# Latent attention on one Trainium2 core: softmax denominators as a product with ones, reciprocals out of PSUM, maxima turned by a product with the identity

## The chip, the cores and the metric

The kernel runs on one core of one Trainium2 chip. The core has a matrix engine (TensorE, PE in the profile; its weight loads are PEld), a vector engine (VectorE, DVE), an activation engine (ScalarE, ACT), a general engine (GpSimd, POOL) and a queue that issues DMAs (SyncE, SP). PE writes only to PSUM, which has eight banks of 512 fp32 columns on 128 partitions; in this kernel POOL works on SBUF, and DVE and ACT read PSUM.

The metric is the device time of one execution in microseconds, as the median of repeated runs. One execution is also profiled; a unit's timeline comes from it.

## The reference, cut to what matters

The model has two layers on 1024 latent and 256 context tokens of width 1024: windowed attention, then multi-head latent attention. The change touches the core of the second layer. It has 16 heads; the scores of a head are the sum of a 64-wide product and a 32-wide rotary product, over 1280 keys (256 context and 1024 latent):

```python
def attend(qn, qr, kn, kr, v):
    s = (jnp.einsum("bqhd,bkhd->bhqk", qn, kn)
         + jnp.einsum("bqhd,bkd->bhqk", qr, kr)).astype(F32) * scale
    p = jax.nn.softmax(s, axis=-1).astype(v.dtype)
    return jnp.einsum("bhqk,bkhd->bqhd", p, v)
...
yx = (ox * jax.nn.silu(gx)) @ w_out
```

The softmax needs each query's maximum before the exponentials and each query's sum after them. The result of a head is multiplied by a gate and goes into the output product.

## The kernel before, in words

**Units.** The second layer's attention runs as 32 units (`UnitB`), one for each head and half of the queries: pair of heads, head `e` in the pair, half, in the order `i = 4 * pair + 2 * e + half`. A unit has 512 queries.

**Steps of a unit.** `prep` loads the unit's queries from DRAM with eight DMAs. `top(b)`, b = 0 to 3, computes the scores of 128 queries against all keys with the queries on the partitions (line 1322 into `psm`, two PSUM banks, for the first 1024 keys; line 1330 into `rest`, columns 256 to 511 of banks 0 and 1, for the last 256 keys, in `top(1)` and `top(2)` only, for two blocks at once), and DVE takes negated maxima (lines 1324, 1331) into one column per block of the tile `mx`; `top(3)` joins the two kinds of maxima (line 1333). `shift` turns the four columns into rows by a PE transpose into `pm_bank` (bank 1, columns 0 to 127; line 1337), and DVE and ACT place them as extra rows of the query operand (lines 1338, 1343). `score(i)`, i = 0 to 4, computes the scores again with 256 keys on the partitions (line 1359, as two products side by side), so that the shifted scores land in one of two two-bank `slots`; `expo` takes the exponential on ACT (line 1365) into a ring of six tiles and POOL adds the tiles up into `acc`, a [128, 512] tile whose sum over partitions is the denominator (lines 1369, 1373). `PV` is the value product (line 1381), ten products of 512 columns whose stationary operand has 64 columns; they go in pairs into the lower and the upper half of the partitions of bank 0 (`pv_bank`). `fin` and `fin1` add the two halves (ACT line 1396, DVE line 1400) into the unit's part of `o`; for e = 1 `fin1` also issues the load of the gate.

**Denominators.** `fin2` turns `acc` by four PE transposes into a bank of a slot (line 1410), so that the queries lie on the partitions, and DVE sums along the free dimension (line 1411). For e = 1 DVE takes the reciprocals of both heads, [128, 8] (line 1414), and ACT spreads them to 64 columns (line 1419). One iteration later, `fin3` turns them back with four transposes (line 1425), DVE multiplies `o` of both heads (line 1426), POOL multiplies with the gate (line 1428), and a DMA stores the result to `og_d` (line 1429).

**Order of work.** PE, ACT and DVE run in the order in which the program is written (`manual_schedule`); each engine takes its instructions strictly in that order. POOL and the SP queue are ordered by the framework. The loop over `ui` staggers three units: in iteration `ui` the unit `u` is scored, its predecessor `pu` gets its value product and finish, and the next two units (`nu`, `nnu`) get their maxima. On PE an iteration is: `score(0)` around `nu.top(2)`, `score(1)`, `nu.top(3)`, in some iterations `make_K` (keys of the next pair, for `ui % 4` of 0 or 1), `pu.PV`, `nu.shift`, `ppu.fin3` (after odd `e`), `pu.fin2`, in iterations 8, 16 and 24 `make_V` (values of the next heads), `nnu.top(0)`, `score(2)`, `score(3)`, `nnu.top(1)`, `score(4)`. On DVE `fin1` stands behind the maximum of `nnu.top(0)` and ahead of that of `nnu.top(1)`; in iterations 8, 16 and 24 it stands ahead of `make_V`. The generators `wo_fill` and `out_fill` place pieces of the output weights' preparation and of the output product, which follows.

Of the kernel before, what the change touches and what calls it, by code (L numbers as in the profile page):

```python
# [14 lines left out]
AX = mybir.AxisListType  # L15
# [32 lines left out]
def shp(ap, *dims):  # L48
    n = 1
    for d in dims:  # L50
        n *= d
    ap = ap[:, 0:n]
    if len(dims) == 1:
        return ap
    names = "abcdefg"[: len(dims)]
    kw = {c: d for c, d in zip(names[1:], dims[1:])}
    return ap.rearrange("p (" + " ".join(names) + ") -> p " + " ".join(names), **kw)
# [3 lines left out]
def kernel(ctx: ExitStack, tc: tile.TileContext, t, out, dbg=None):  # L61
    nc = tc.nc
# [4 lines left out]
    PB = ppool.tile([128, 8, 512], F32, name="PB")  # L67
    R = cpool.tile([128, int(R_KB * KB)], F32R, name="arena_r")
    F = cpool.tile([128, F_KB * KB], F32, name="arena_f")
    ident = cpool.tile([128, 128], F32, name="ident")  # L70
# [21 lines left out]
    def f_at(kb, *dims):  # L92
        n = int(np.prod(dims))
        return shp(F[:, int(kb * KB) : int(kb * KB) + n], *dims)
# [177 lines left out]
    sm_ring8 = SmallRing(6, 8)  # L272
# [279 lines left out]
    rbr = Ring(F, [42, 47], 256)  # L552
# [26 lines left out]
    class UnitA:  # L579
# [96 lines left out]
        def fin2(self, fast=False):  # L676
            g, og = self.g, self.og
            o = self.o
            rt = shp(prt(), 4, 128)
            for j in range(2):  # L680
                nc.tensor.transpose(rt[:, j, :], self.rb[:, j * 128 : j * 128 + 128], ident)
            rs = shp(rtr.next(), 2, 128)
            nc.scalar.copy(rs, rt[:, 0:2, :])
            eng = nc.vector if fast else nc.gpsimd
            eng.tensor_mul(rs, rs, self.gt)
            eng.tensor_mul(o, o, rs)
            hi = og[:, 0, 2 * g : 2 * g + 2, :]
            eng.tensor_copy(hi, o)
            eng.tensor_sub(og[:, 1, 2 * g : 2 * g + 2, :], o, hi.bitcast(F32))  # L689
# [23 lines left out]
    units = [UnitA(ti, g) for ti in ORDER for g in range(4)]  # L713
# [46 lines left out]
    class RawRing:  # L760
        i = 5

        def next(self):
            self.i += 1
            return raw[:, self.i - 1, :]
# [104 lines left out]
    for c in range(2):  # L870
        ps = proj_t(1, 0, c)
# [14 lines left out]
    for bi in (8, 9):  # L886
        for c in range(2):
            ps = proj_t(bi, 0, c)
# [268 lines left out]
    for ti in range(NT):  # L1157
        n = ti + 3
# [50 lines left out]
    glr = Ring(R, [60, 62], 512)  # L1209
    warm = sm(1)  # L1210
    otr = Ring(F, [0, 4], 1024)
    rbr = Ring(F, [8, 9], 256)
    mxr = Ring(F, [44, 44.5], 128)
    psm = PB[:, 2:4, :]
    pm_bank = PB[:, 1, 0:128]
    slots = [PB[:, 4:6, :], PB[:, 6:8, :]]
    pv_bank = PB[:, 0, :]
    rest = PB[:, 0:2, 256:512]

    def slot():  # L1220
        slots.reverse()
        return slots[1]
# [67 lines left out]
    class UnitB:  # L1290
# [43 lines left out]

        def shift(self):
            pm, r2 = pm_bank, self.q[2]
            nc.tensor.transpose(pm[0:100], self.mx[:, 0:100], ident)
            nc.vector.tensor_mul(
                shp(r2[32:36], 4, 128),
                pm[32:36].unsqueeze(1).to_broadcast([4, 4, 128]),  # L1340
                ident[32:36, 32:36].unsqueeze(2).to_broadcast([4, 4, 128]),
            )
            nc.scalar.copy(r2[96:100], r2[32:36].bitcast(F32))
# [41 lines left out]
        def fin(self):  # L1385
            if self.e == 0 and self.half == 0:
                UnitB.o = shp(otr.next(), 2, 512)
                UnitB.dens = {}
            if self.e == 0:
                UnitB.dens[self.half] = shp(sm_ring8(), 2, 4)  # L1390
            self.den = UnitB.dens[self.half]
            self.o = UnitB.o[:, self.half, :]
            pv = self.pv
            a, b2 = (slice(0, 64), slice(64, 128)) if self.e == 0 else (slice(64, 128), slice(0, 64))
            self.a = a
            nc.scalar.copy(self.o[a], pv[b2])
# [7 lines left out]
                    out=self.gt.bitcast(F32), in_=g1_d[self.pair, :, self.half * 512 : self.half * 512 + 512]  # L1404
                )

        def fin2(self, pd):
            pd = shp(pd, 4, 128)
            for b in range(4):
                nc.tensor.transpose(pd[:, b, :], self.acc[:, b * 128 : b * 128 + 128], ident)  # L1410
            nc.vector.reduce_sum(self.den[:, self.e, :], pd, AX.X)
            if self.e == 0:
                return
            nc.vector.reciprocal(self.den, self.den)
            rec = self.den.rearrange("p e b -> p b e").unsqueeze(3)
            self.rbs = []
            for b in range(0, 4, 2):
                rb = shp(rbr.next(), 2, 2, 64)
                nc.scalar.copy(rb, rec[:, b : b + 2].to_broadcast([128, 2, 2, 64]))
                self.rbs.append(rb)  # L1420

        def fin3(self, rt):
            for b in range(4):
                rb = self.rbs[b // 2][:, b % 2].rearrange("p e d -> p (e d)")
                nc.tensor.transpose(rt[:, b * 128 : b * 128 + 128], rb, ident)
            nc.vector.tensor_mul(self.o, self.o, rt)
            eng = nc.vector if self.i == NU - 1 else nc.gpsimd
            eng.tensor_mul(self.o, self.o, self.gt.bitcast(F32))
            load(out=og_d[self.pair, :, self.half * 512 : self.half * 512 + 512], in_=self.o)
# [114 lines left out]
    units = [UnitB(i) for i in range(NU)]  # L1544
    vk = make_V(0, slots[0], slots[1])
    for m in mxr.bufs:
        nc.vector.memset(m, 0.0)
    for p in range(1, 3):
        g_tile(8, p)
    g_tile(9, 1)  # L1550
# [7 lines left out]
    with tc.manual_schedule(engines={E.PE, E.Activation, E.DVE}):  # L1558
        kr = make_kr()
        ones_kr()  # L1560
        next(kr)
        next(kr)
        g_tile(8, 3, 0, pv_bank)
        next(kr)
        g_tile(8, 3, 1)
        make_K(0, (0, 1), slot())
        g_tile(9, 3, 0, psm[:, 0])
        make_K(0, (2,), slot())
        g_tile(9, 3, 1)
        next(vk)  # L1570
        u0.top(0)
        next(vk)
        g_tile(8, 4, 0, slots[0][:, 0])
        u0.top(1)
        next(vk)
        u0.top(2)
        g_tile(8, 4, 1)
        units[2].prep()
        u0.top(3)
        g_tile(9, 4, 0, slots[0][:, 1])  # L1580
        u0.shift()
        u1.top(0)
        make_K(1, (0, 2), slots[1])
        u1.top(1)
        g_tile(9, 4, 1)
        nc.scalar.activation(warm, const[:, 1:2], AF.Exp)
        u1.top(2)
        for ui, u in enumerate(units):
            pu, ppu = [units[ui - n] if ui >= n else None for n in (1, 2)]
            nu, nnu = [units[ui + n] if ui + n < NU else None for n in (1, 2)]  # L1590
            if nnu and ui:
                nnu.prep()
            if ui == 0:
                u.score(0)
                nu.top(3)
                u.score(1)
                nu.shift()
                nnu.top(0)
                u.score(2)
                u.score(3)  # L1600
                nnu.top(1)
                u.score(4)
                continue
            u.score(0, 0, 2)
            if nu:
                nu.top(2)
            u.score(0, 2, 5)
            u.score(1, hold=True)
            if nu:
                nu.top(3)  # L1610
            x = slot()
            if ui % 4 == 0 and u.pair < 7:
                make_K(u.pair + 1, (0, 2), x)
            if ui % 4 == 1 and u.pair < 7:
                make_K(u.pair + 1, (1,), x)
            if ui == NU - 2:
                next(out_fill)
            pu.PV()
            u.expo(1)
            if ui % 4 > 1 and ui < 23 or ui > 25:  # L1620
                next(wo_fill)
            if ui == NU - 1:
                next(out_fill)
            pu.fin()
            if nu:
                nu.shift()
            if ppu and ppu.e == 1:
                ppu.fin3(x[:, 0])
            pu.fin2(x[:, 1])
            if ui % 8 == 0:  # L1630
                pu.fin1()
                for _ in make_V(u.pair // 2, x):
                    pass
            if nnu:
                nnu.top(0)
            if ui % 8:
                pu.fin1()
            u.score(2)
            u.score(3)
            if nnu:  # L1640
                nnu.top(1)
            u.score(4)
        u, pu = units[-1], units[-2]
        pu.fin3(slot()[:, 0])
        next(out_fill)
        next(out_fill)
        u.PV()
        u.fin()
        u.fin1()
        next(out_fill)  # L1650
        next(out_fill)
        u.fin2(slot()[:, 0])
        next(out_fill)
        next(out_fill)
        u.fin3(slot()[:, 0])
    for _ in out_fill:
        pass

# [73 lines left out]
```

## Time and profile before

| | |
|---|---|
| median of 3 runs | 1577.26 us (1575.3 to 1577.57) |
| the profiled execution's own time | 1574.73 us |
| its span | 1573.0 us |
| granted TensorE clock, mean | 0.995 |
| PE busy | 1538.7 us, 98% |
| DVE busy | 993.5 us, 63% |
| ACT busy | 772.8 us, 49% |
| POOL busy | 753.8 us, 48% |

A line of a group in the profile names the source line, the engine, the operation, the tiles written and read, shapes and count; then the busy time, the mean duration of one in ns, and the idle time of the engine just ahead of it with what ended it. `PB` is PSUM, `arena_f`, `arena_r` and `arena_k` are SBUF. A timeline line has the start in us, the length in us, engine, line and operation; neighbouring equal instructions are merged (x4), and idle time ahead stands in brackets. Many lines share line 128 to 130, the helper for products split into three.

### The profile page before, as it was taken

What the parts mean: (1) busy time and instruction counts of PE and PEld (TensorE: products, weight loads), DVE (VectorE), ACT (ScalarE), POOL (GpSimd) and SP (SyncE); (2) the same over time, 40 slices, a digit from 0 to 9 for tenths busy, and PEclk for the clock granted to TensorE, in tenths of its full rate; (3) what the DMA queues carried; (4) which work ended last, traced back from release to release, by engine and by line L of the source; (5) the groups of instructions that cost most, each with busy time, mean ns of one, the idle gap of its engine ahead of it and who ended that gap; (6) DMA issues with size and microseconds to landing.
All of it is one profiled execution on the core that took longest, in us unless ns stands there. A gap on an engine that the chain in (4) does not pass through costs nothing.

```text
span 1573.0 us, 26868 instructions
## 1 busy us (share of the span) xinstructions
PE 1538.7 (98%) x9846; PEld 1228.6 (78%) x9846; DVE 993.5 (63%) x1757; ACT 772.8 (49%) x1492; POOL 753.8 (48%) x810
## 2 busy tenths in 40 slices
PE   7999999999999999998999999999999999999998
PEld 4988888887878888888998899666766766766687
DVE  3878996657777777768425203666567566567354
ACT  4432322267777777767313323455555555555322
POOL 1151211136564444544105140588688688689410
PEclk9999999999999999999999999999999999999999
DMA  8357774653343222345105753313233233244251
GB/s 316 114 159 219 199 207 137 200 164 99 99 146 100 85 89 85 95 132 182 48 1 156 262 151 98 91 45 98 61 98 101 71 91 88 61 138 113 69 168 68
DMA packets 148277, 192.83 MB, mean 123 GB/s; under 512 B 13985, under 2 KB 86177, under 8 KB 148145
## 3 DMA queue, kind: packets, MB, share of 16 engines
q1 hardware_dynamic: 146672, 188.94, 40.2%
q10 hardware_dynamic: 1472, 2.16, 0.5%
q8 instruction: 78, 1.28, 0.3%
q14 instruction: 55, 0.44, 0.1%
HBM read 144.90 MB, written 46.15 MB: 121 GB/s over the span
## 4 chain that ended last, share of the span: by engine, by line
PE 81%; DVE 8%; issue 3%; DMA 3%; ACT 2%; POOL 2%; SPq 0%; DVEq 0%; POOLq 0%; ACTq 0%
PE PB L128 12%; PE PB L129 12%; PE PB L130 12%; PE PB L1359 12%; PE PB L1381 9%; PE PB L621 5%; PE PB L662 5%; PE PB L1322 4%; PE PB L652 4%; DVE arena_f L193 2%; DVE arena_f L519 1%; DMA arena_f<-a_w_in 1%; PE PB L1330 1%; PE PB L1410 1%; ACT arena_r L123 1%
## 5 line engine op out<-in xcount | busy, mean ns | idle before, releaser
L128 PE MATMUL PB<-arena_r 128*128 128x512 f32 (+3 forms) x1216 | 410.8, 339 | 5.5 <-ACT arena_r L423 2.4
L129 PE MATMUL PB<-arena_r 128*128 128x512 f32 (+3 forms) x1184 | 395.2, 334 | 1.8 <-POOL arena_r L689 0.8
L130 PE MATMUL PB<-arena_r 128*128 128x256 f32 (+3 forms) x1152 | 381.5, 332 | 0.2 <-DVE arena_r L124 0.2
L1373 POOL TENSOR_TENSOR arena_f<-arena_f 128x512 f32<-128x512 f32 x252 | 324.9, 1289 | 79.7 <-ACT arena_f L1365 62.9
L128 PEld LDWEIGHTS PB<-arena_r 128*128 128x128 f32 x1216 | 231.1, 191 | 32.2 <-ACT arena_r L423 4.8
L129 PEld LDWEIGHTS PB<-arena_r 128*128 128x128 f32 x1184 | 226.4, 191 | 22.9 <-DVE arena_r L424 2.4
L124 POOL TENSOR_TENSOR arena_r<-arena_f,arena_r 128x512 fp32r<-128x512 f32 x80 | 109.3, 1381 | 276.8 <-ACT arena_r L123 226.8
L130 PEld LDWEIGHTS PB<-arena_r 128*128 128x128 f32 x1152 | 220.4, 191 | 20.7 <-issue 1.7
L1365 ACT ACTIVATE arena_f<-PB 128x1024 f32<-128x1024 f32 x160 | 164.1, 1027 | 108.5 <-PE PB L1359 68.4
L1324 DVE TENSOR_REDUCE arena_f<-PB 128x1 f32<-128x1024 f32 x128 | 156.0, 1219 | 86.7 <-PE PB L1322 86.6
L1359 PE MATMUL PB<-arena_r 64*128 64x512 f32 (+1 forms) x1500 | 195.1, 392 | 0.3 <-ACT arena_f L1365 0.3
L1359 PEld LDWEIGHTS PB<-arena_r 64*128 64x128 f32 (+1 forms) x1500 | 137.1, 185 | 28.9 <-ACT arena_f L1365 1.8
L124 DVE TENSOR_TENSOR arena_r<-PB,arena_r 128x512 fp32r<-128x512 f32 x168 | 114.6, 689 | 61.1 <-ACT arena_r L123 60.2
L1381 PE MATMUL PB<-arena_f 128*64 128x512 f32 x640 | 144.4, 597 | 0.0
L632 DVE CUSTOM_DVE_ANT_0 arena_f<-PB,arena_f,small 128x640 f32<-128x640 f32 (+2 forms) x176 | 125.2, 722 | 19.5 <-PE PB L621 11.6
L635 ACT ACTIVATE arena_f<-arena_f,small 128x640 f32<-128x640 f32 (+2 forms) x160 | 119.5, 747 | 35.1 <-DVE small L632 32.6
L123 ACT CAST arena_r<-PB 128x512 fp32r<-128x512 f32 x176 | 101.7, 585 | 46.6 <-PE PB L652 44.6
L621 PE MATMUL PB<-arena_k,arena_r 128*128 128x256 f32 (+1 forms) x576 | 111.2, 308 | 1.5 <-DVE small L632 1.3
L1381 PEld LDWEIGHTS PB<-arena_f 128*64 128x64 f32 x640 | 43.1, 136 | 83.2 <-issue 79.9
L652 PE MATMUL PB<-ident,arena_f 128*128 128x128 f32 x672 | 104.0, 274 | 0.6 <-DVE arena_r L124 0.3
L123 ACT CAST arena_r<-arena_f 128x512 fp32r<-128x512 f32 (+2 forms) x121 | 72.0, 605 | 62.1 <-DMA arena_f<-a_w_in 14.5
L621 PEld LDWEIGHTS PB<-arena_k,arena_r 128*128 128x128 f32 x576 | 89.2, 189 | 13.9 <-DVE small L632 3.5
(213 smaller groups left out, 2532.5 us busy)
## 6 DMA issues: line engine op xcount, KB each, us to landing
arena_f<-ada_w SPq DMA_DIRECT2D x40, 512.0 KB, 4.8
arena_r<-q_d SPq DMA_DIRECT2D x80, 256.0 KB, 4.1
arena_r<-qn_d SPq DMA_DIRECT2D x64, 256.0 KB, 4.0
arena_r<-qr_d SPq DMA_DIRECT2D x172, 64.0 KB, 3.4
arena_f<-a_w_in SPq DMA_DIRECT2D x40, 256.0 KB, 3.1
g_d<-arena_f SPq DMA_DIRECT2D x32, 256.0 KB, 2.6
q_d<-arena_f SPq DMA_DIRECT2D x64, 128.0 KB, 2.5
qn_d<-arena_f SPq DMA_DIRECT2D x16, 512.0 KB, 5.3
```

The costliest lines, as they stand in the source:

```text
L123: nc.scalar.copy(hi, src)
L124: (lo_eng or nc.vector).tensor_sub(lo, src, hi.bitcast(F32))
L128: nc.tensor.matmul(o, ah, bh, start=first, stop=False)
L129: nc.tensor.matmul(o, al, bh, start=False, stop=False)
L130: nc.tensor.matmul(o, ah, bl, start=False, stop=last)
L621: nc.tensor.matmul(S[:, at : at + n], qT[:, s, hq, :], kT[:, g, k : k + n], start=s == 0, stop=s == 1)
L652: nc.tensor.transpose(pt[:, h, :], self.Ps[h][:, ci * 128 : ci * 128 + 128], ident)
L1324: nc.vector.reduce_max(mx[:, 32 + b : 33 + b], flat, AX.X, negate=True)
L1359: nc.tensor.matmul(S[:, t], k[r, c : c + 128], q[r], start=j == 0, stop=j == 4)
L1365: nc.scalar.activation(E, self.S, AF.Exp)
L1373: eng.tensor_add(self.acc, self.acc, E[:, t])
L1381: nc.tensor.matmul(self.pv[p : p + 64], Vq[:, cs[t], self.h % 4, :], E[:, t], start=i == 0, stop=i == 4)
```

## The change

The denominators are no longer turned. `fin2` multiplies a [128, 64] tile of ones with `acc` in two products of 256 columns, one into partitions 0 to 63 and one into 64 to 127 of `den` (bank 1, columns 256 to 511), directly behind `PV`. Each of the 64 rows then holds the sums. `fin3` moves into the same iteration, behind `fin1`: DVE takes the reciprocals out of PSUM in two instructions of [64, 256] into `rec` and multiplies the unit's own half of `o`; for e = 1 the gate's product and the store follow. The transposes, the sum, the small reciprocal and the ACT copies go, and with them the spare `slot()` in iterations without `make_K`. `shift` is a product with the identity as the moving operand and 64 columns of `mx` as the stationary one, in place of a transpose of 100 columns. In iterations 8, 16 and 24 `fin1` and `fin3` stand ahead of `make_V`. In the last unit, `fin2` follows `PV` at once, into a slot.

```diff
-    rbr = Ring(F, [8, 9], 256)
+    ones = f_at(51, 64)
+    rec = f_at(8, 512)
...
+    den = PB[:, 1, 256:512]
...
         def shift(self):
             pm, r2 = pm_bank, self.q[2]
-            nc.tensor.transpose(pm[0:100], self.mx[:, 0:100], ident)
+            nc.tensor.matmul(pm[0:64], self.mx[:, 0:64], ident, start=True, stop=True)
...
-        def fin2(self, pd):
-            pd = shp(pd, 4, 128)
-            for b in range(4):
-                nc.tensor.transpose(pd[:, b, :], self.acc[:, b * 128 : b * 128 + 128], ident)
-            nc.vector.reduce_sum(self.den[:, self.e, :], pd, AX.X)
+        def fin2(self, ps=den):
+            self.den = ps
+            for t in range(2):
+                nc.tensor.matmul(
+                    ps[64 * t : 64 * t + 64], ones, self.acc[:, 256 * t : 256 * t + 256], start=True, stop=True
+                )
+
+        def fin3(self):
+            a = self.a
+            for t in range(2):
+                nc.vector.reciprocal(rec[a, 256 * t : 256 * t + 256], self.den[64 * t : 64 * t + 64])
+            nc.vector.tensor_mul(self.o[a], self.o[a], rec[a])
             if self.e == 0:
                 return
-            nc.vector.reciprocal(self.den, self.den)
...
-                nc.scalar.copy(rb, rec[:, b : b + 2].to_broadcast([128, 2, 2, 64]))
...
-        def fin3(self, rt):
-            for b in range(4):
...
-                nc.tensor.transpose(rt[:, b * 128 : b * 128 + 128], rb, ident)
-            nc.vector.tensor_mul(self.o, self.o, rt)
             eng = nc.vector if self.i == NU - 1 else nc.gpsimd
             eng.tensor_mul(self.o, self.o, self.gt.bitcast(F32))
...
-            x = slot()
-            if ui % 4 == 0 and u.pair < 7:
-                make_K(u.pair + 1, (0, 2), x)
-            if ui % 4 == 1 and u.pair < 7:
-                make_K(u.pair + 1, (1,), x)
+            if ui % 4 < 2 and u.pair < 7:
+                x = slot()
+                make_K(u.pair + 1, (1,) if ui % 4 else (0, 2), x)
...
+            pu.fin2()
             pu.fin()
             if nu:
                 nu.shift()
-            if ppu and ppu.e == 1:
-                ppu.fin3(x[:, 0])
-            pu.fin2(x[:, 1])
             if ui % 8 == 0:
                 pu.fin1()
+                pu.fin3()
                 for _ in make_V(u.pair // 2, x):
                     pass
             if nnu:
                 nnu.top(0)
             if ui % 8:
                 pu.fin1()
+                pu.fin3()
             u.score(2)
             u.score(3)
             if nnu:
                 nnu.top(1)
             u.score(4)
-        u, pu = units[-1], units[-2]
-        pu.fin3(slot()[:, 0])
+        u = units[-1]
...
         u.PV()
+        u.fin2(slot()[:, 0, 0:256])
         u.fin()
...
-        u.fin2(slot()[:, 0])
...
-        u.fin3(slot()[:, 0])
+        u.fin3()
```

More of the change, by code (lines that the diff above doesn't have):

```diff
@@ L1387, in fin @@
                 UnitB.o = shp(otr.next(), 2, 512)
[L1388 to L1391, printed above, removed]
             self.o = UnitB.o[:, self.half, :]
@@ L1405, in fin1 @@
                 )
-        def fin2(self, pd):
-            pd = shp(pd, 4, 128)
-            for b in range(4):
-                nc.tensor.transpose(pd[:, b, :], self.acc[:, b * 128 : b * 128 + 128], ident)
-            nc.vector.reduce_sum(self.den[:, self.e, :], pd, AX.X)
+        def fin2(self, ps=den):
[9 more added lines that the diff above has]
+            nc.vector.tensor_mul(self.o[a], self.o[a], rec[a])
             if self.e == 0:
                 return
[L1414 to L1418, printed above, removed]
-                nc.scalar.copy(rb, rec[:, b : b + 2].to_broadcast([128, 2, 2, 64]))
-                self.rbs.append(rb)
-        def fin3(self, rt):
-            for b in range(4):
-                rb = self.rbs[b // 2][:, b % 2].rearrange("p e d -> p (e d)")
-                nc.tensor.transpose(rt[:, b * 128 : b * 128 + 128], rb, ident)
-            nc.vector.tensor_mul(self.o, self.o, rt)
             eng = nc.vector if self.i == NU - 1 else nc.gpsimd
@@ L1547 @@
         nc.vector.memset(m, 0.0)
+    nc.vector.memset(ones, 1.0)
     for p in range(1, 3):
@@ L1588 @@
         for ui, u in enumerate(units):
-            pu, ppu = [units[ui - n] if ui >= n else None for n in (1, 2)]
+            pu = units[ui - 1]
             nu, nnu = [units[ui + n] if ui + n < NU else None for n in (1, 2)]
```

## The prediction

> **What bounds the kernel now.** I read the page's totals first, then busy time by stretch, then the timeline of one unit of the latent attention, whose 32 units run from about 980 to 1489 us. Columns of the second view: stretch, length, busy time (instructions) of each engine, granted clock, DMA share, GB/s.
>
> ```profile
> PE 1538.7 (98%) x9846; PEld 1228.6 (78%) x9846; DVE 993.5 (63%) x1757; ACT 772.8 (49%) x1492; POOL 753.8 (48%) x810
> ```
>
> ```profile
> 1040.00:1480.00 440.00, 439.40 (x3164) 288.75 (x3164) 283.18 (x373) 230.70 (x303) 354.83 (x271) 1.00 0.32 88
> ```
>
> TensorE (PE) is busy for 439.4 of 440 us, DVE for 283 and POOL for 355. In this stage every microsecond that PE waits is paid, and work of another engine counts only where PE waits for it. The unit's timeline (start, us, engine, line) shows how close DVE stands to that:
>
> ```profile
> 1159.48 4.51 PE L1381 MATMUL PB<-arena_f 128*64 128x512 f32 x20
> ...
> 1163.93 0.32 PE L1337 MATMUL PB<-ident,arena_f 128*100 128x128 f32 x1
> ...
> 1164.08 0.60 PE L1410 MATMUL PB<-ident,arena_f 128*128 128x128 f32 x4
> ...
> 1164.28 0.68 DVE L1338 TENSOR_TENSOR arena_r<-PB,ident 4x512 fp32r<-4x512 f32 x1 [1.22 <-PE PB L1337]
> ...
> 1164.61 0.73 PE L1322 MATMUL PB<-arena_r 64*128 64x512 f32 x4
> ...
> 1165.00 0.69 DVE L1411 TENSOR_REDUCE small<-PB 128x4 f32<-128x512 f32 x1
> ...
> 1165.18 2.47 PE L1359 MATMUL PB<-arena_r 64*128 64x512 f32 x20
> 1165.72 0.20 DVE L1414 RECIPROCAL small<-small 128x8 f32<-128x8 f32 x1
> 1165.84 1.17 DVE L1324 TENSOR_REDUCE arena_f<-PB 128x1 f32<-128x1024 f32 x1
> ...
> 1167.05 0.69 DVE L1400 TENSOR_TENSOR arena_f<-PB,arena_f 64x512 f32<-64x512 f32 x1
> ...
> 1167.49 0.63 PE L1322 MATMUL PB<-arena_r 64*128 64x512 f32 x4
> 1167.79 8.11 POOL L1373 TENSOR_TENSOR arena_f<-arena_f 128x512 f32<-128x512 f32 x6 [0.87 <-ACT arena_f L1365]
> ...
> 1167.96 0.40 PE L1330 MATMUL PB<-arena_r 64*128 64x256 f32 x4
> ...
> 1168.16 1.23 DVE L1324 TENSOR_REDUCE arena_f<-PB 128x1 f32<-128x1024 f32 x1 [0.42 <-PE PB L1322]
> 1168.20 1.81 PE L1359 MATMUL PB<-arena_r 64*128 64x512 f32 x14
> 1169.09 1.16 SPq L1308 DMA_DIRECT2D arena_r<-qn_d  x2
> 1169.31 0.68 DVE L1331 TENSOR_REDUCE arena_f<-PB 128x2 f32<-128x512 f32 x1
> ...
> 1169.84 0.63 PE L1322 MATMUL PB<-arena_r 64*128 64x512 f32 x4
> ...
> 1170.31 0.40 PE L1330 MATMUL PB<-arena_r 64*128 64x256 f32 x4
> ```
>
> PE runs value product (L1381), transposed maxima (L1337), four transposes for the denominators (L1410), `top(0)` (L1322), `score(2)` and `score(3)` (L1359), then `top(1)` (L1322, L1330). DVE follows in its written order: L1338, denominator sum and reciprocal (L1411, L1414), maximum of `top(0)` (L1324), `fin1` (L1400), maximum of `top(1)`. DVE ends L1400 at 1167.74 and PE writes L1330, into the same PSUM bank that L1400 reads, at 1167.96. DVE has 0.2 us to spare there.
>
> **The change, part by part.**
>
> PE, each unit. From the first value product to the first `top(0)` product it takes 1164.61 - 1159.48 = 5.13 us. The value product is 20 instructions of 512 columns in 4.45 us (to 1163.93), 0.445 us for each of its ten side-by-side pairs of passes. The ones product is two such pairs at 256 columns, 0.445; the maxima's product is two passes of 128 columns with no partner, 0.22, with some weight load showing, 0.25. The way into another tile form, which the old transposes paid on both sides, is paid once, about 0.1. Sum 4.35 + 0.445 + 0.25 + 0.1 = 5.15 us. I count 0, give or take 0.1 a unit (3 us over 32).
>
> PE, each second unit: `fin3`'s four transposes go.
>
> ```profile
> 1179.86 0.60 PE L1425 MATMUL PB<-ident,arena_f 128*128 128x128 f32 x4
> ...
> 1180.29 0.60 PE L1410 MATMUL PB<-ident,arena_f 128*128 128x128 f32 x4
> ```
>
> From these to the next four is 0.43 us, on the path; 16 x 0.43 = 6.9 us gained.
>
> DVE, each unit, loses L1411 (0.69) and shares of L1414 and L1426 and gains two reciprocals of 64x256 out of PSUM and one 64x512 product (as L1400, 0.69). The trace has no reciprocal of that size. The nearest rows:
>
> ```profile
> L1414 DVE RECIPROCAL small<-small 128x8 f32<-128x8 f32 x16 | 3.3, 204 | 0.5
> ```
>
> ```profile
> L1284 DVE TENSOR_TENSOR arena_r<-PB,arena_r 64x256 fp32r<-64x256 f32 x32 | 13.5, 422 | 3.7 <-ACT arena_r L1286 2.5
> L211 DVE TENSOR_TENSOR small<-PB,small 128x8 f32<-128x8 f32 x7 | 1.1, 162 | 8.8 <-PE PB L203 8.8
> L1015 DVE TENSOR_SCALAR small<-small 128x1 f32<-128x1 f32 x18 | 2.7, 151 | 38.9 <-ACT arena_f L1014 38.9
> ```
>
> Other DVE instructions take 151 ns at one element, 162 ns at 8, 422 ns at 256: some 150 ns plus 1.05 ns an element. The reciprocal of 8 takes 204 ns. If the extra 42 ns is a fixed cost, 256 elements take 0.42 to 0.47 us: the lower bound. If it goes with the elements, it is 5.3 ns each: 154 + 256 x 6.3 ns = 1.77 us; with the whole 54 ns above 150 put on 8 elements it is 1.88, the upper bound. Operations of different kinds share the same 150 to 160 ns at small sizes, so I see no reason for a fixed extra and take 1.77. [...]
>
> Where this lies: `fin3` stands on DVE ahead of `top(1)`'s maximum, and the ones product sits in bank 1, columns 256 to 511, which L1330 of `top(1)` overwrites. So PE cannot pass L1330 until both reciprocals are read. In the times of the quoted unit, with D for one reciprocal: the maxima's product now follows the ones product, so L1338 starts 0.445 plus a weight load later, at 1164.75, and and ends 1165.43; L1324, 1.22, ends 1166.69; L1400 ends 1167.41; the reciprocals end at 1167.47 + 2D, 1171.0 for D = 1.77. L1330 starts at 1171.07 in place of 1167.96: **PE stands 3.1 us**. Next late is the product (to 1171.73), then L1324 (1172.98) and L1331 (1173.69). PE's next L1322, 1.88 us after L1330, waits 0.1 for the one, the next L1330 0.24 for the other. Together 3.4 us, or 2D - 0.1. After that DVE has the 4.45 us of the value product to catch up.
>
> It happens in each iteration with a `top(1)`: 1 to 29, without 8, 16 and 24, where `make_V`, ten tiles of products, stands between and hides it. 26 x 3.4 = 88 us.
>
> What a stand of 3.1 us does to TensorE's clock. Stretches cut at the 3.41 us in which the granted clock changes:
>
> ```profile
> 16.27:19.68 3.41, 2.09 (x15) 1.69 (x13) 1.49 (x3) 1.36 (x3) 1.27 (x1) 1.00 1.05 394
> 19.68:23.10 3.42, 3.40 (x16) 3.10 (x16) 1.53 (x5) 2.66 (x5) 0.60 (x2) 0.50 1.06 408
> 33.34:36.75 3.41, 1.75 (x8) 1.13 (x8) 1.73 (x5) 3.41 (x8) 0.55 (x1) 1.00 0.86 292
> 36.75:40.16 3.41, 2.90 (x14) 2.90 (x15) 2.70 (x8) 2.85 (x7) 0.55 (x1) 0.50 0.99 362
> 446.37:449.78 3.41, 2.13 (x12) 1.53 (x11) 2.27 (x6) 2.46 (x7) 2.63 (x6) 1.00 0.14 49
> 449.78:453.20 3.42, 3.42 (x20) 2.65 (x19) 3.11 (x9) 2.54 (x9) 1.84 (x3) 1.00 0.55 147
> 722.83:726.24 3.41, 1.74 (x11) 1.29 (x10) 2.97 (x7) 2.51 (x5) 2.18 (x3) 1.00 0.39 141
> 726.24:729.66 3.42, 2.75 (x14) 2.40 (x13) 1.73 (x8) 2.46 (x9) 1.77 (x3) 0.50 0.85 251
> 729.66:733.07 3.41, 3.41 (x16) 3.39 (x15) 2.81 (x4) 2.42 (x5) 3.37 (x4) 0.50 0.48 153
> ```
>
> A stretch with PE busy for 1.74 to 2.09 of 3.41 us is followed by one or two at clock 0.50; with 2.13 us (446.37) it is not. Whatever the phase, a 3.1 us stand leaves one of two neighbouring stretches at least 1.55 us empty, so busy for 1.86 or less. At half clock 3.41 us do 1.7 us less work. Over the phases: 1.7 where the stand lies mostly ahead of the cut's end; 1.4 where its rest falls into the slow stretch, and then, as at 726.24, often a second slow one. I take 2.0 us a stand (1.4 to 3.1); the later waits of 0.3 vanish in it. 26 x (3.1 + 2.0) = 133 us.
>
> [...]
>
> Beside other work, at nothing: ACT loses L1419; PE never waited for it here. Without the spare `slot()` the scores wait less, but PE had no gap to give back. POOL's gate product (L1428) moves one unit ahead and now waits for the DVE product and for the `g1_d` load just issued. Behind it queue the adds (L1373, from 1167.79, 8.11 us) that the ones product needs at the end of the next value product. Held until 1173 they would end near 1179; that product ended just ahead of 1179.86 and ends, with the stand, at about 1183: covered; without cover it costs 1.3 us at 16 places, 21 us. Behind the `og_d` store on SP's queue stand the next loads (L1308 on), held by some 4 us; their unit's `top(0)` comes only after the next value product.
>
> The tail: the last gate product of the unit before the last comes earlier.
>
> ```profile
> 1477.78 1.27 POOL L1428 TENSOR_TENSOR arena_f<-arena_f,arena_r 128x512 f32<-128x512 f32 x1 [3.77 <-DVE arena_f L1426]
> ...
> 1479.07 0.33 SPq L1429 DMA_DIRECT2D og_d<-arena_f  x1
> ...
> 1487.95 0.19 PEld L129 LDWEIGHTS PB<-arena_r,arena_k 128*128 128x128 f32 x1 [1.07 <-DVE arena_k L124]
> ```
>
> The store leaves before the last value product rather than in it, and the wait of 1.07 us ahead of L129 goes: with 0.2 for a form change I count 1.3 us. **Sum:** 133 - 6.9 - 1.3 = +124 us on the profiled execution's 1574.7 (span 1573.0), that is 1699; the median of the three runs shown is 2.5 above it, so 1701.
>
> **The rivals.**
>
> 1. The stands come but the clock holds: 88 - 8.2 = +80, 1657. For it: the 2.13 us stretch stands close to the bound. Against: three stretches as empty as these lost the clock. Chance 0.23.
>
> 2. The reciprocal passes at the plain rate, D = 0.42 to 0.47: 2D - 0.1 is 0.74 to 0.84 us a unit, 26 x 0.74 - 8.2 = +11, 1588. L1338's later start and the product are enough to make DVE late at L1330. The clock holds. Chance 0.10.
>
> 3. Faster: DVE is through before PE comes to L1330, and only PE's 8.2 us are left: 1569. The place is L1330's wait again; it decides where 26 x (2D - 0.1) falls under 8.2, at D = 0.21 (or where the maxima's product and `top(0)` come 0.4 us sooner). For it: DVE is busy for only 64% of the stage. Against: no DVE row reads 256 elements in under 0.42. Chance 0.07.
>
> 4. The reciprocals take 2.2 us or more, or POOL's gate product holds the adds as well: about 1725 to 1790. Chance 0.06.
>
> **How the numbers follow.** My forecast, slow reciprocals and a falling clock, has 0.54 and lies between 1677 (D = 1.6, the clock costing 1.4 us a stand) and 1736 (D = 1.88, 3.1 us). With rival 1, down to 1650 at D = 1.6, that is 0.77; the range takes in half of rival 4 as well: 1640 to 1760. 0.2%, 3 us, is what a measurement of this kernel can tell. Faster by more comes from rival 3, 0.07; no change, 0.04, from the fast edge of rival 2; the rest, 0.89, is slower.
>
> **What would show it.** RECIPROCAL 64x256 near 1770 ns (450 ns would be rival 2). PE's idle time ahead of L1330 put down to a DVE reciprocal, some 80 us in 26 places; L1322 waiting on L1324 hardly more than now. Granted clock near 0.9 in the stage, with stretches of 3.41 us at 0.50 right after the stands (1.00 throughout would be rival 1). First L1381 to first L1322 at 5.1 to 5.2 us. Iterations 8, 16 and 24 as long as before. The prediction is wrong if L1330 doesn't wait, or if POOL's L1373 ends after the value product that needs it.

## The result, and the profile after

| | before | after |
|---|---|---|
| median (lowest to highest) | 1577.41 us (1575.30 to 1579.20), 4 runs | 1692.66 us (1685.57 to 1694.96), 4 runs |
| profiled execution, its span | 1574.73, 1573.0 us | 1694.96, 1693.1 us |
| granted clock of that execution | 0.995 | 0.969 |

The ratio is 1.0721 (95% interval 1.0700 to 1.0742), 115 us more at the median. The forecast was 1701 (1640 to 1760), slower. The profiled execution of after is the longest of its four; its terms below are taken against its own span, 120.1 us above that of before.

The source view of the value product gives its first and last start. Before (first row, before), then after (second row):

```profile
L1381 PE MATMUL PB<-arena_f x640: 592/592/644, 1008.0 to 1480.6; 128*64 128x512 f32 x160
```

```profile
L1383 PE MATMUL PB<-arena_f x640: 592/592/644, 1012.1 to 1602.3; 128*64 128x512 f32 x160
```

Between these starts lie 472.6 us before and 590.2 after: 117.6 of the 120.1 us are in the 31 iterations between value products. 4.1 us lie ahead of the first value product, and the stretch behind the last start is 1.6 us shorter (92.4 against 90.8).

The page of after, its totals and three of its groups, and the stage in the view of busy time by stretch (stretch, length, busy time and instructions of PE, PEld, DVE, ACT, POOL, granted clock, DMA share, GB/s):

```profile
PE 1586.8 (94%) x9814; PEld 1278.7 (76%) x9814; DVE 1119.9 (66%) x1790; ACT 762.9 (45%) x1460; POOL 759.1 (45%) x810
...
L1415 DVE RECIPROCAL arena_f<-PB 64x256 f32<-64x256 f32 x64 | 112.2, 1753 | 0.9
...
L1332 PE MATMUL PB<-arena_r 64*128 64x256 f32 x256 | 44.3, 349 | 69.5 <-DVE arena_f L1415 69.5
```

```profile
1020.00:1568.00 548.00, 475.23 (x3117) 332.90 (x3117) 399.71 (x403) 218.74 (x270) 356.96 (x271) 0.92 0.25 69
```

In this stage PE was busy for all but 0.6 us of 440 before; now it is idle for 548.0 - 475.2 = 72.8 us, and 69.5 us of idle time stand ahead of L1332 (before: L1330) because of the reciprocal. The granted clock is 0.92. The view of waits says how often and for how long:

```profile
PEld PB L1332 <- DVE arena_f L1415: 77.8, 26, 3.1
...
PE PB L1332 <- DVE arena_f L1415: 69.5, 26, 2.8
```

26 stands, 3.0 us each by the weight load's row, 2.7 by the product's. The timeline of one unit whose clock held (lines: start, us, engine, line):

```profile
1187.58 4.51 PE L1383 MATMUL PB<-arena_f 128*64 128x512 f32 x20
...
1191.92 0.60 PE L1408 MATMUL PB<-arena_f 128*64 128x256 f32 x4
...
1192.66 0.73 PE L1324 MATMUL PB<-arena_r 64*128 64x512 f32 x4
...
1192.77 0.68 DVE L1340 TENSOR_TENSOR arena_r<-PB,ident 4x512 fp32r<-4x512 f32 x1 [1.01 <-PE PB L1339]
...
1193.48 1.23 DVE L1326 TENSOR_REDUCE arena_f<-PB 128x1 f32<-128x1024 f32 x1
...
1194.74 0.68 DVE L1398 TENSOR_TENSOR arena_f<-PB,arena_f 64x512 f32<-64x512 f32 x1
...
1195.35 3.51 DVE L1415 RECIPROCAL arena_f<-PB 64x256 f32<-64x256 f32 x2
...
1196.03 0.28 PE L1332 MATMUL PB<-arena_r 64*128 64x256 f32 x1
1198.89 1.46 DVE L1416 TENSOR_TENSOR arena_f<-arena_f 64x512 f32<-64x512 f32 x1
...
1198.91 0.50 PE L1332 MATMUL PB<-arena_r 64*128 64x256 f32 x3 [2.61 <-DVE arena_f L1415]
...
1200.39 1.23 DVE L1326 TENSOR_REDUCE arena_f<-PB 128x1 f32<-128x1024 f32 x1
...
1201.67 0.73 PE L1324 MATMUL PB<-arena_r 64*128 64x512 f32 x4 [0.62 <-DVE arena_f L1326]
```

The reader is to see three things. PE needs 1192.66 - 1187.58 = 5.08 us from the value product to `top(0)`, as before (5.13). The first product of L1332 runs, since it goes into bank 0; the next goes into bank 1, columns 256 to 511, which is `den`, and waits until both reciprocals have read it. And the product L1416 takes 1.46 us, twice what it was priced at, so the next L1324 waits 0.62 us for the maximum behind it.

The granted clock, in stretches cut at its changes, behind three of the stands:

```profile
1133.03:1136.44 3.41, 1.41 (x13) 0.91 (x9) 3.37 (x3) 1.83 (x2) 2.38 (x2) 1.00 0.00 0
1136.44:1139.85 3.41, 2.67 (x14) 2.67 (x16) 3.34 (x4) 0.00 (x0) 3.25 (x4) 0.50 0.00 0
1139.85:1143.27 3.42, 3.42 (x21) 3.42 (x19) 1.91 (x3) 1.02 (x1) 2.82 (x3) 0.50 0.33 105
...
1194.48:1197.89 3.41, 1.82 (x17) 1.23 (x13) 3.37 (x4) 2.06 (x2) 1.97 (x2) 1.00 0.00 0
1197.89:1201.30 3.41, 2.13 (x17) 1.70 (x17) 3.34 (x3) 0.60 (x1) 3.25 (x3) 1.00 0.00 0
...
1232.02:1235.43 3.41, 1.45 (x13) 0.94 (x9) 3.37 (x3) 1.88 (x2) 2.33 (x2) 1.00 0.00 0
1235.43:1238.84 3.41, 2.62 (x14) 2.62 (x16) 3.34 (x4) 0.00 (x0) 3.25 (x4) 0.50 0.00 0
1238.84:1242.26 3.42, 3.42 (x21) 3.42 (x20) 1.91 (x3) 1.02 (x1) 2.82 (x3) 0.50 0.26 98
```

Twice a stretch with PE busy for 1.41 and 1.45 us is followed by two at 0.50. After 1.82 us, inside the bounds that the prediction had drawn (1.74 to 2.09 falls), it is not. The same view over all stretches between the first and the last value product is sharper: 21 stretches at full clock with PE busy for 0.66 to 1.58 us are followed by a fall, and none of those with 1.71 us or more. So in this stage the fall begins near half of 3.41 us. Between the first and the last value product the clock's records show 21 slow episodes for the 26 stands, 15 of 3.41 us and 6 of 6.83: 92 us in all. An estimate from these figures: a stand of 2.7 us, placed at any phase, leaves one stretch more than half empty in 2.7 of 3.4 cases, 20 or 21 of 26.

### The profile page after: what moved, and what is told of

It is laid out like the page before. It is cut to its first block, busy times and chain, and to the rows that moved or that the text cites. A ratio compares the mean times of both kernels' runs of the same rounds, so it can differ in the third digit from the quotient of the medians.

```text
span 1693.1 us, 26749 instructions
## 1 busy us (share of the span) xinstructions
PE 1586.8 (94%) x9814; PEld 1278.7 (76%) x9814; DVE 1119.9 (66%) x1790; ACT 762.9 (45%) x1460; POOL 759.1 (45%) x810
## 3 DMA queue, kind: packets, MB, share of 16 engines
q10 hardware_dynamic: 1472, 2.16, 0.5%
## 4 chain that ended last, share of the span: by engine, by line
PE 74%; DVE 17%; issue 4%; ACT 2%; POOL 1%; DMA 1%; SPq 0%; DVEq 0%; POOLq 0%; ACTq 0%
PE PB L128 12%; PE PB L129 12%; PE PB L130 12%; PE PB L1361 8%; PE PB L1383 8%; DVE arena_f L1415 6%; PE PB L621 4%; PE PB L662 4%; PE PB L652 4%; PE PB L1324 3%; DVE arena_f L1326 2%; DVE arena_f L193 2%; PE PB L1332 2%; DVE arena_f L1398 1%; DVE arena_f L519 1%
## 5 line engine op out<-in xcount | busy, mean ns | idle before, releaser
L1375 POOL TENSOR_TENSOR arena_f<-arena_f 128x512 f32<-128x512 f32 x252 | 336.4, 1335 | 178.8 <-ACT arena_f L1367 165.5
L129 PE MATMUL PB<-arena_r 128*128 128x512 f32 (+3 forms) x1184 | 395.4, 334 | 1.8 <-POOL arena_r L689 0.8
L129 PEld LDWEIGHTS PB<-arena_r 128*128 128x128 f32 x1184 | 226.9, 192 | 23.1 <-DVE arena_r L424 2.9
L1361 PE MATMUL PB<-arena_r 64*128 64x512 f32 (+1 forms) x1500 | 231.4, 435 | 0.2
L1361 PEld LDWEIGHTS PB<-arena_r 64*128 64x128 f32 (+1 forms) x1500 | 178.1, 212 | 19.8 <-ACT arena_f L1367 1.4
L1383 PE MATMUL PB<-arena_f 128*64 128x512 f32 x640 | 144.4, 597 | 0.0
L1415 DVE RECIPROCAL arena_f<-PB 64x256 f32<-64x256 f32 x64 | 112.2, 1753 | 0.9
L1332 PE MATMUL PB<-arena_r 64*128 64x256 f32 x256 | 44.3, 349 | 69.5 <-DVE arena_f L1415 69.5
L1383 PEld LDWEIGHTS PB<-arena_f 128*64 128x64 f32 x640 | 43.1, 136 | 83.3 <-issue 80.0
```

The lines of the kernel that those rows point to most:

```text
L129: nc.tensor.matmul(o, al, bh, start=False, stop=False)
L1361: nc.tensor.matmul(S[:, t], k[r, c : c + 128], q[r], start=j == 0, stop=j == 4)
L1375: eng.tensor_add(self.acc, self.acc, E[:, t])
L1383: nc.tensor.matmul(self.pv[p : p + 64], Vq[:, cs[t], self.h % 4, :], E[:, t], start=i == 0, stop=i == 4)
L1415: nc.vector.reciprocal(rec[a, 256 * t : 256 * t + 256], self.den[64 * t : 64 * t + 64])
```

## The experiments

How the units are compared: the interval from the first instruction of one value product (L1381 or L1383) to that of the next is one iteration; for each kernel its change against before, summed over iterations 1 to 27, over 28 and 29, and what a single iteration changes. Iterations 8, 16 and 24 are apart. All but the first row are experiments told of below.

| kernel | iterations 1 to 27 | 28 and 29 | one of the 24 others | 8, 16, 24 each |
|---|---|---|---|---|
| after | +108.1 us | +9.4 | +3.5 to +5.9 | -0.28 |
| idle products at the stand | +91.4 | +14.9 | +3.5 to +4.1 | -0.28 |
| one reciprocal in place | +72.2 | +4.8 | +1.6 or +2.0; +3.2 or +3.6 to +3.8 | -0.28 |
| copies for reciprocals | +26.1 | +7.0 | +0.8 or +1.3 | -0.28 |
| no reciprocal, no product | -5.6 | +2.1 | -0.5 or 0.0 | -0.28 |
| maxima alone | +3.0 | +0.1 | +0.1 | +0.1 |
| reciprocals later, first place | -5.6 | -0.4 | -0.5 or 0.0 | -0.28 |
| reciprocals later, second place | +17.3 | +0.2 | 0.0 to +3.4 | +2.1 |

Where a row gives two values with "or", the lower is that of iterations in which before had `fin3`'s four transposes (9 of the 24). The experiments are told in the order of the theories that they part: first the reciprocal's rate, then the clock, then the size of the work, then PE's own share, then the place.

### Copies for reciprocals

```diff
-                nc.vector.reciprocal(rec[a, 256 * t : 256 * t + 256], self.den[64 * t : 64 * t + 64])
+                nc.vector.tensor_copy(rec[a, 256 * t : 256 * t + 256], self.den[64 * t : 64 * t + 64])
```

> The changed kernel with the two reciprocals replaced by copies of the same shape out of PSUM (the division is left out: the outputs are multiplied by the sums). Theory of the prediction: the copies take 0.42 us each in place of 1.75, the stand ahead of the products into rest shrinks from 3.0 to about 0.4 us, the slower 64x512 product that the trace of the change shows (1.3 us) keeps the next maximum late by some 0.7, and the clock holds at 0.99 or more: 1590 to 1610 us. Rival (order and tile forms of the change cost a good part of the 115 us by themselves): it stays above 1640 us.

Measured: 1608.97 us (1607.10 to 1610.14), ratio to before 1.0197 (1.0176 to 1.0219). Two groups of its page and two waits:

```profile
L1415 DVE COPY arena_f<-PB 64x256 f32<-64x256 f32 x64 | 26.8, 419 | 0.9
...
L1416 DVE TENSOR_TENSOR arena_f<-arena_f 64x512 f32<-64x512 f32 x32 | 40.4, 1262 | 1.1
```

```profile
PEld PB L1324 <- DVE arena_f L1326: 26.4, 27, 1.3
...
PEld PB L1332 <- DVE arena_f L1415: 8.5, 25, 0.6
```

The copy takes 419 ns where the reciprocal takes 1753, and 84 of the 115 us are gone: the rate of the reciprocal carries the larger part. The change is slower all the same, since the product (1262 ns) delays the maximum that the next L1324 waits for, by 1.0 us in 27 places. The edit also shows a cost that the prediction had put at nothing: iterations 28 and 29 are 7 us longer, where PE waits for queries. The queue's and PE's rows in that unit:

```profile
1465.87 0.34 SPq L1421 DMA_DIRECT2D og_d<-arena_f  x1
...
1468.74 1.16 SPq L1310 DMA_DIRECT2D arena_r<-qn_d  x2
...
1474.59 0.49 PE L1324 MATMUL PB<-arena_r 64*128 64x512 f32 x1 [0.29 <-DMA arena_r<-qn_d]
```

The loads of L1310 go out on SP's queue 2.9 us behind the store of the unit's result (L1421), and `top(0)` of their unit waits for them. In before they follow the store by the same 2.9 us (1430.64 to 1433.57), but the store leaves 5.4 us ahead of the next value product, and here 3.3. In after itself these two iterations, at +4.1 and +5.3, look like the rest.

### Idle products at the stand

Eleven pairs of products that nobody reads, into a free slot, between `top(1)`'s first products and L1332, in the 26 iterations whose `top(1)` had stood:

```diff
+            for _ in range(11 if fill else 0):
+                for t in range(2):
+                    r = slice(64 * t, 64 * t + 64)
+                    nc.tensor.matmul(slots[0][:, t], fill.kt[r, 0, 0:128], fill.q[0][r, 0], start=True, stop=True)
...
-                nnu.top(1)
+                nnu.top(1, u if ui % 8 else None)
```

> The changed kernel with 11 pairs of idle products (64x128 by 64x512, into the score slot that is free at that time, never read) put on PE at the place of the stand, 2.6 us of work into a wait of 3.0. PE has more to do and never stands for more than half a us, so the clock should stay at full speed. Theory of the prediction with its 2.0 us a stand for the clock: 1640 to 1650 us. The reading of the trace of the change (units without a slow stretch are longer by 3.9 us, those with one by 4 to 6): the clock is worth 15 to 20 us, 1670 to 1680. Rival (the clock costs nothing, its slow stretches lie under DVE's chain): 1690 us or more.

Measured: 1682.94 us (1679.83 to 1684.94), ratio 1.0667 (1.0647 to 1.0687). That is far above the 1640 to 1650 of the prediction's 2.0 us a stand, and 3 us above the 1670 to 1680 read from the trace of after. Timeline at one stand (L1330 is the added product, L1336 and L1419 are after's L1332 and L1415), and the stage:

```profile
1204.70 3.53 DVE L1419 RECIPROCAL arena_f<-PB 64x256 f32<-64x256 f32 x2
...
1205.25 2.66 PE L1330 MATMUL PB<-arena_r 64*128 64x512 f32 x22
...
1208.26 1.38 DVE L1420 TENSOR_TENSOR arena_f<-arena_f 64x512 f32<-64x512 f32 x1
1208.28 0.50 PE L1336 MATMUL PB<-arena_r 64*128 64x256 f32 x3 [0.26 <-DVE arena_f L1419]
...
1210.95 0.50 PE L1324 MATMUL PB<-arena_r 64*128 64x512 f32 x2 [0.54 <-DVE arena_f L1326]
```

```profile
1020.00:1558.00 538.00, 514.06 (x3695) 344.81 (x3693) 400.33 (x405) 217.94 (x270) 357.96 (x271) 0.99 0.26 71
```

PE is now busy through the stand and the clock is 0.99 in the stage; in iterations 1 to 27 no stretch at 0.50 is left. DVE still sets the end of the stand. Adding work to PE made the kernel 10 us faster than after: in iterations 1 to 27 the clock had cost 108.1 - 91.4 = 16.7 us, of which iterations 28 and 29, where PE waits for queries as it did with the copies, give back 5.4 (14.9 - 9.4). What remains without it, 3.5 to 4.1 us an iteration, is stand and later waits, less PE's gain.

### One reciprocal in place, products out of PSUM

```diff
+            nc.vector.reciprocal(self.den, self.den)
             for t in range(2):
-                nc.vector.reciprocal(rec[a, 256 * t : 256 * t + 256], self.den[64 * t : 64 * t + 64])
-            nc.vector.tensor_mul(self.o[a], self.o[a], rec[a])
+                cs = slice(256 * t, 256 * t + 256)
+                nc.vector.tensor_mul(self.o[a, cs], self.o[a, cs], self.den[64 * t : 64 * t + 64])
```

> The changed kernel with one reciprocal over 128 partitions by 256 columns, in place in PSUM, and two products of 64x256 that read it from PSUM. Theory (the cost goes with the elements of a partition): the one instruction takes 1.75 us like each of the two before, the chain on DVE is 1.75 + 0.84 in place of 3.5 + 1.3, the stand falls from 3.0 to about 2.1 us and the wait after it to about nothing; with fewer slow stretches 1635 to 1660 us. Rival (the cost goes with all elements or with the rows): one instruction of 3.5 us and 1675 us or more.

Measured: 1656.92 us (1655.08 to 1657.88), ratio 1.0502 (1.0484 to 1.0521). Its groups and the wait:

```profile
L1414 DVE RECIPROCAL PB<-PB 128x256 f32<-128x256 f32 x32 | 56.2, 1757 | 0.5
...
L1417 DVE TENSOR_TENSOR arena_f<-arena_f,PB 64x256 f32<-64x256 f32 x64 | 26.8, 419 | 1.5
```

```profile
PEld PB L1332 <- DVE arena_f L1417: 55.1, 26, 2.2
```

128 rows take 1757 ns, 64 rows 1753: the reciprocal's time goes with the elements of one partition, so two instructions on 64 rows each paid double. The products out of PSUM take 419 ns each, 0.84 for what took 1.3 out of SBUF. The stand is 2.1 us, and no wait of L1324 follows.

The intervals also show what a fall of the clock costs where nothing hides it: 1.6 or 2.0 us without a slow stretch, 3.2 or 3.6 with one of 3.41 us, so 1.6 us each. In after the same single stretch costs 0.4 to 0.9 us, because PE's slow work lies where it would have waited for DVE's maximum in any case: ahead of L1324 PE is idle for 0.5 to 0.6 us in the five iterations that kept the clock, and for nothing in those that lost it, but for 0.28 us in one. Only two stretches in a row cost 1.8.

### No reciprocal and no product

```diff
         def fin3(self):
             a = self.a
-            for t in range(2):
-                nc.vector.reciprocal(rec[a, 256 * t : 256 * t + 256], self.den[64 * t : 64 * t + 64])
-            nc.vector.tensor_mul(self.o[a], self.o[a], rec[a])
```

> The changed kernel without the reciprocals and without the product that uses them (the outputs are not divided by the sums); products with ones, maxima's product and order stay. Theory: no stand, and PE's side of the change alone shows: the 8.2 us that the prediction counts as gained, 1567 to 1571 us. Rival (the new forms cost PE as much as the transposes that went): 1576 to 1580 us, as before.

Measured: 1570.56 us (1568.78 to 1572.61), ratio 0.9956 (0.9941 to 0.9971): 6.65 us for PE's side alone. An iteration is 0.04 us shorter where nothing but the forms changed (in some 0.01 longer), and 0.5 shorter where `fin3`'s transposes had stood. 2.1 us are lost again in iterations 28 and 29.

### The maxima's product alone, in the kernel before

```diff
-            nc.tensor.transpose(pm[0:100], self.mx[:, 0:100], ident)
+            nc.tensor.matmul(pm[0:64], self.mx[:, 0:64], ident, start=True, stop=True)
```

> The kernel before with one part of the change alone: shift is a product with the identity in the 64-column form, the four transposes of fin2 still follow it. Theory: the form is now kept from the value product to the maxima's product and changed behind it, so one change of form moves and none goes; two passes of 128 columns replace one transpose, 0.1 us a unit: 1577 to 1582 us. Rival (staying in the form saves a change of form of 0.1 to 0.2 us a unit): 1571 to 1574 us.

Measured: 1581.27 us (1578.61 to 1583.32) beside 1578.60, ratio 1.0020 (1.0011 to 1.0030), 0.11 us a unit. Between transposes the new form costs a little; in the change, the ones product and the maxima's product together cost no more than what they replace (the kernel above). No run shows the two apart there.

### Reciprocals one iteration later

Two kernels that keep the ones product and the maxima's product, exchange the places of `den` and `pm_bank` in bank 1 (so that no L1332 overwrites `den`), use the one reciprocal in place, and take it with its products out of the stretch ahead of `top(1)`: one iteration later, behind the maximum of `nu.top(3)`. In the first kernel this is ahead of `make_K`; the second has the two added lines behind `pu.PV()` and `u.expo(1)` instead, behind `make_K` and under the value product:

```diff
-    pm_bank = PB[:, 1, 0:128]
+    pm_bank = PB[:, 1, 256:384]
...
-    den = PB[:, 1, 256:512]
+    den = PB[:, 1, 0:256]
...
             if nu:
                 nu.top(3)
+            if ui > 1:
+                units[ui - 2].fin3()
...
             if ui % 8:
                 pu.fin1()
-                pu.fin3()
+                if ui == NU - 1:
+                    pu.fin3()
```

> A version that keeps PE's gain and takes the reciprocal off the path: the sums go to bank 1, columns 0 to 255, which no top() writes, the turned maxima to columns 256 to 383; the reciprocal is one instruction of 128x256 in place, and it and the two products of 64x256 out of PSUM run one iteration later, on DVE behind the maximum of nu.top(3) and ahead of make_K's copies, under the value product. Theory: DVE needs 1.2 + 0.2 + 1.75 + 0.84 and 0.7 to 3.3 for its other work there, 4.7 to 7.3 us, and PE gives it 5.4 to 7.7 us until the turned maxima are ready; no stand, the clock holds, the SP queue as before: 1567 to 1573 us, faster than both kernels. Rival (the bank is shared, and PE's products into bank 1 or DVE's chain still wait): 1580 us or more.

> As e7a_defer, with the reciprocal and the products behind make_K's copies on DVE instead of ahead of them. Theory: in the iterations with make_K the order inside the value product's cover changes, not the sum; within 3 us of e7a_defer. Rival (the turned maxima come late because DVE waits for ACT's part of make_K's copies first): 5 to 15 us slower than e7a_defer.

Measured for the first: 1568.34 us (1566.66 to 1569.59) beside 1578.60, ratio 0.9941 (0.9928 to 0.9954): faster than both kernels, by 10 us (0.6%) against before. Its page and one unit on DVE:

```profile
PE 1531.4 (98%) x9814; PEld 1223.5 (78%) x9814; DVE 1039.3 (66%) x1790; ACT 763.4 (49%) x1460; POOL 753.1 (48%) x810
...
L1414 DVE RECIPROCAL PB<-PB 128x256 f32<-128x256 f32 x32 | 56.1, 1753 | 0.0
```

```profile
1144.79 1.23 DVE L1326 TENSOR_REDUCE arena_f<-PB 128x1 f32<-128x1024 f32 x1 [0.74 <-PE PB L1324]
...
1146.20 1.75 DVE L1414 RECIPROCAL PB<-PB 128x256 f32<-128x256 f32 x1
1147.99 0.85 DVE L1417 TENSOR_TENSOR arena_f<-arena_f,PB 64x256 f32<-64x256 f32 x2
...
1149.87 0.68 DVE L1340 TENSOR_TENSOR arena_r<-PB,ident 4x512 fp32r<-4x512 f32 x1 [0.44 <-PE PB L1339]
```

The reciprocals cost the same 56 us of DVE as in the kernel with one reciprocal in place, and none of it reaches the end: PE is idle for neither, DVE itself waits for PE ahead of L1340. Iterations 1 to 27 are those of the kernel without any reciprocal, to 0.01 us, and 28 and 29 together are no longer than in before.

Measured for the second: 1595.05 us (1594.03 to 1597.49), ratio 1.0113 (1.0097 to 1.0129). It is slower by more than either theory had expected. One unit with `make_K` ahead of it:

```profile
1056.41 2.56 DVE L1286 TENSOR_TENSOR arena_r<-PB,arena_r 64x512 fp32r<-64x512 f32 x5
...
1058.98 1.77 DVE L1414 RECIPROCAL PB<-PB 128x256 f32<-128x256 f32 x1
...
1060.78 0.85 DVE L1417 TENSOR_TENSOR arena_f<-arena_f,PB 64x256 f32<-64x256 f32 x2
...
1061.78 1.00 PE L1408 MATMUL PB<-arena_f 128*64 128x256 f32 x4 [2.16 <-DVE arena_f L1417]
```

In iterations with `make_K` the keys' subtractions (L1286) hold DVE until 1058.97, and the reciprocal and its products follow. They still read `den` when PE is done with the value product, and the next ones product (L1408) would overwrite it: PE stands 2.16 us until L1417 has ended. The view of waits has 12 such places, one for each iteration with `make_K` and a `fin3`:

```profile
PE PB L1408 <- DVE arena_f L1417: 19.0, 12, 2.2
```

That is most of the 22.9 us by which iterations 1 to 27 are longer than in the first kernel. Only the place differs from it.

## Why the prediction was right

The direction, the range and the mechanism held. The forecast's 1701 is 8 us above the median. That is closer than its terms were, and so in part luck: the clock was priced too high and the waits behind the stand too low, and the two errors stood against each other.

**What held.** The reciprocal: predicted 1.77 us, measured 1.753 (1.737 to 1.762). The extrapolation from the 204 ns row, with all of the extra put on the elements, was right. The stand: predicted 3.1 us in 26 places, measured 3.0 in 26. Iterations 8, 16 and 24: as predicted not longer (-0.28). PE's 5.15 us from the value product to `top(0)`: 5.08. L1340 runs 0.11 us behind the start of L1324 where it had started 0.33 ahead: 0.44 late, predicted 0.47. POOL's adds were in time, as PE stood ahead of the ones product for 0.4 us in all:

```profile
L1408 PE MATMUL PB<-arena_f 128*64 128x256 f32 x128 | 19.3, 380 | 0.4 <-POOL arena_f L1375 0.4
```

The tail: 1.6 us, predicted 1.3, though the wait ahead of L129 that was to go only fell, from 1.07 to 0.62 us; what made up the rest isn't shown.

**The product, mis-sized.** The term "one 64x512 product (as L1400, 0.69)" was the step that failed. L1400 reads one of its operands from PSUM; the product reads both from SBUF, while POOL adds in SBUF. Its group in after, and its last case in the timeline, behind the last value product, where POOL has nothing to add:

```profile
L1416 DVE TENSOR_TENSOR arena_f<-arena_f 64x512 f32<-64x512 f32 x32 | 41.7, 1303 | 1.1
```

```profile
1615.32 0.69 DVE L1416 TENSOR_TENSOR arena_f<-arena_f 64x512 f32<-64x512 f32 x1
```

It took 1303 ns in the mean and 0.69 us there. The trace has 32 of them: the four that overlap no instruction of POOL take 0.69 us each, and of the 28 beside POOL's adds (L1375) 27 take 1.32 to 1.53 us and one 0.95. The prediction had not weighed where the operands lie and what POOL does meanwhile. The rows: 1.32 to 1.53 us with both operands in SBUF beside POOL, 0.69 us with POOL idle; with one operand in PSUM 0.67 to 0.70 us for all 32 of L1400 in before, two of which lie wholly beside an instruction of POOL, and 2 x 419 ns (each 411 to 425) in the kernel with one reciprocal in place. So the later waits, predicted at 0.3 us a stand, which were to "vanish" in the clock's cost, are 1.0: the idle-product kernel's 91.4 us less the -5.6 of PE's side are 97.0 in 24 places, 4.04 each, of which 3.0 are the stand. That is 0.64 us more than the 3.4 of rival 1's sum, 17 us over 26 places, and 0.94 more than the 3.1 that the forecast's own sum holds beside the clock, 24 us. The sign "L1322 waiting on L1324 hardly more than now" did not come: where the clock held, PE stands 0.5 to 0.6 us there.

**The clock, mis-sized the other way.** Predicted 2.0 us a stand, 52 in all; measured 16.7 us over the 24 stands of iterations 1 to 27, 0.7 each. The clock does fall after stands that leave a stretch more than half empty, here 21 times (PE busy for 0.66 to 1.58 us of 3.41). But the price was worked out as if PE's slow work were all on the path. It isn't: the waits that the long product causes lie right behind the stand, and slow products fill them. Five of the 24 iterations kept the clock and show no loss at all. The bound of 2.1 us was too high for this stage: stretches of 1.71 and 1.82 kept the clock. That the fall's price is 1.6 us where no wait follows (one reciprocal in place) bears the explanation out; it is close to the 1.7 us that the prediction gave as the lost work.

**PE's gain, a little too high.** 8.2 us predicted (6.9 and 1.3), 6.65 measured without the division. The units gave what was priced (0.43 to 0.49 where `fin3` had stood, but 0.28 in iterations 8, 16 and 24); iterations 28 and 29 took back 2.1, where "held by some 4 us" behind the store on SP's queue had been put down as covered.

**The sum again, with what was measured:** 24 stands at 4.04 + 0.70 = 113.8, less 5.6 for PE's side (with iterations 8, 16 and 24 in it), is 108.1 for iterations 1 to 27. Iterations 28 and 29 add 9.4, the last two nothing, the stretch ahead of the first value product 4.1, the tail -1.6: 120.0 of 120.1 us. The 4.1 us ahead of the first value product were not predicted and stay unexplained: the seven kernels of the experiments show between 0.5 and 5.4 there. After and the first four of them run the same instructions up to that point and show 1.9 to 5.2, so much of it may be scatter between executions.

**The rivals.** Rival 1 (the clock holds, 1657) had the wrong clock, and would have had the wrong time with the right one: the kernel whose clock holds takes 1683. Rival 2's mechanism, tried with copies, gives 1609 and not 1588, by the product's length and the queue. Rival 3's 1569 is reached when DVE is out of the way, by the first of the two later kernels, at 1568.3. Rival 4 did not come: no run shows a reciprocal of 2.2 us (1.762 at most in after), and POOL's adds weren't late.

## What to carry to other kernels

Ahead of a DVE reciprocal, count the elements of one partition: from 204 ns at 8 and 1753 at 256 it is about 154 ns + 6.25 ns an element here, and the same at 256 for 64 rows and for 128, so a form that leaves eight elements on a partition may be worth its transposes. Then read what stands behind it in the engine's order and who overwrites the PSUM place that it reads: the same 56 us of reciprocals stand between 1656.9 and 1568.3 us here, by their place alone in DVE's order and in the bank (the two were moved together). When a stand of PE is priced, put the waits that follow it first and the lost clock into what they leave over.

## What the runs showed of the hardware that was not expected

- A 64x512 product of two SBUF tiles takes 1.3 us in the mean in a stage where POOL is busy for two thirds, and 0.69 in the four cases without POOL; with one operand in PSUM, as two instructions, 0.84.
- Work for nobody on PE, 22 products in 2.66 us, made the kernel 10 us faster than leaving PE idle.
- The clock fell to 0.50 with no wholly idle stretch (the emptiest had PE busy for 0.66 us). In the attention stage of after all full-clock stretches of 3.41 us with PE busy for 1.58 us or less lost it and all with 1.71 or more kept it; with one reciprocal in place the two sides are 1.69 and 1.75, but for one stretch of 2.06 that lost it, behind the last stand. That is near half of the stretch. It isn't settled for other work: stretches of 1.74 to 2.09 us had lost it in other stages of the kernel before.
